# Sparse attention: the two heads of an output tile handled as one unit, their matmuls alternating

## The chip, the cores and the metric

The kernel runs on one core of one Trainium2 chip. The metric is the device time of the program in microseconds (us); lower is better.

## The reference, cut to what matters

The program is one layer of a decoder trunk on 256 tokens of width 2048 in float32: a first feed-forward, a mixer of three branches (a short gated convolution, a sparse attention, a cross-attention into 256 memory tokens), an output projection, and a second feed-forward. The part that the change touches is the sparse attention. It has 16 heads of width 64 in 4 groups. Each head adds up three gated terms:

```
p_c = masked_softmax(q . k_c * scale)          # 15 compressed keys
o_s = softmax(q . k_sel * scale) . v_sel       # selected blocks: at 256 tokens all of them, causal
o_w = softmax(q . k_win * scale) . v_win       # window: at 256 tokens the full causal prefix
o   = g0 * (p_c . v_c) + g1 * o_s + g2 * o_w   # sigmoid gates
```

At this length both the selected branch and the window branch are full causal attention over 256 tokens, with different keys and values.

## The kernel before, in words

**The main stream.** All projections are streams of 128x128 weight tiles, eight to a chunk (512 KB). `Stream.fetch` (L134 to L144) loads a chunk as `wraw`; ScalarE rounds it to `whi` (L143), VectorE takes the rest as `wlo` (L144). `proj` (L213) then issues two matmuls for each weight tile into a PSUM tile `psw` of two banks: `whi` against 512 columns (L232, both halves of the operand) and `wlo` against 256 columns (L233). `evac` (L238) empties `psw` with one ScalarE and one VectorE instruction.

**Side work.** Everything else runs as Python generators that are stepped between weight tiles. A `tick` (L203) first advances each active generator by one step, in order, and then takes the next one from `queue` and runs its first step. `proj` calls `tick` at fixed places of a group of weight tiles. While the sparse attention is computed, the stream goes through 32 groups of 24 weight tiles (gate and branch projections of the convolution and memory branches, L820 to L834); three groups of four have one tick at their end, and the fourth has one in its middle and one at its end. So ticks lie 24 or 12 weight tiles apart. When the program is built, a scheduler orders the instructions of each engine by their place in the program and by when it reckons their operands to be ready. The order on each engine is fixed from then on.

**The sparse attention.** Head pairs: output tile j (of 8) holds two heads, g = 0 on partitions 0 to 63 and g = 1 on 64 to 127. For each j, branch and g there is one `causal_unit` (L637), 32 in all. Its first step makes the scores into one bank (tag "sc", one buffer), with two matmuls that read 64 partitions: 128 columns for the first 128 tokens (L645), 256 for the others (L646). Mask and maximum on VectorE (L652, L655), exponent on ScalarE (L657), and the scaling on VectorE (L660 to L663) follow. The second step, a tick later, transposes the three 128x128 blocks (L667, bank tag "pt", two buffers) and copies them out (`T`, L669). The third, another tick later, adds the values into a half of the partitions of `on` (tag "o"), with one matmul of 256 columns (L672) and one of 128 (L673). For the first unit of an output tile, `begin` (L681) starts `on` with the compressed branch for both heads (L685). The fourth unit of a tile splits `on` into operand parts. `comp_attention` (L605), four in all, makes the compressed probabilities of four heads: eight score matmuls of 15 columns (L613), a small softmax, and in its second step two transposes (L633).

A float32 matmul appears in the trace as two passes, each a weight load and a matmul instruction, so L645 x2 is one matmul. A transpose is one pass.

At a tick in the steady state three units are in work, so TensorE gets: values of one, transposes of the next, scores of a third, and then goes on with the stream.

Of the kernel before, what the change touches and what calls it, by code (L numbers as in the profile page):

```python
# [17 lines left out]
P = 128  # L18
S = 256
# [13 lines left out]
def order(group, late):  # L33
    """(member, k tile, first, last) of a group of output tiles; the last `late` k tiles come last for all,
    or all members take turns ("k")."""
    out = []
    if late == "k":
        n = len(group[0])
        out = [(j, kts[i], i == 0, i == n - 1) for i in range(n) for j, kts in enumerate(group)]
    elif late:  # L40
        for j, kts in enumerate(group):
            out += [(j, k, i == 0, False) for i, k in enumerate(kts[:len(kts) - late])]
        for j, kts in enumerate(group):
            rest = kts[len(kts) - late:]
            out += [(j, k, False, i == late - 1) for i, k in enumerate(rest)]
    else:
        for j, kts in enumerate(group):
            out += [(j, k, i == 0, i == len(kts) - 1) for i, k in enumerate(kts)]
    return out
# [41 lines left out]
def cuts(n, ramp=()):  # L91
    """(first tile, tiles) of the chunks of a stream of n tiles; small ones first where nothing is loaded yet."""
# [14 lines left out]
# columns of the packed parameters  # L107
# [39 lines left out]
class Trunk:  # L147
    def __init__(self, ctx, tc, a):
# [18 lines left out]
        # the tensor engine's clock rises while the first loads are on their way  # L167
# [26 lines left out]
    def spawn(self, gen):  # L194
        """Start side work at once; each further step comes with a tick."""
# [17 lines left out]
    def proj(self, stream, group, late, X, ticks=0, before=None, fold=False):  # L213
        """PSUM tiles [128, 2 members, 512]: (Wh + Wl) @ hi in the first half, Wh @ lo in the second
        (or in the first too, with `fold`)."""
# [31 lines left out]
    def split(self, src, pool=None, tag="h", scale=None):  # L247
        """hi / lo parts of src as a tile [128, 2, 256]."""
# [13 lines left out]
    def norm_parts(self, x, pr, gain, pool, tag):  # L262
        """Operand parts of gain * x for k tiles 2pr, 2pr + 1."""
        return [self.split(x[:, j, :], pool, tag, scale=self.p(gain, 2 * pr + j)) for j in range(2)]

    def norm_sum(self, x):
        """The running sum of squares."""
# [13 lines left out]
    def norm_end(self):  # L281
        """r = rsqrt(mean square + eps): token-major [128, 2] and spread over partitions [128, 256]."""
# [26 lines left out]
    def head_scale(self, ps, out, r, width, post):  # L309
        """out = post * r * rsqrt(r^2 * ss / width + eps), all [128 tokens, 2, n]; ss in PSUM."""  # L310
# [12 lines left out]
    def squares(self, t, fold=False):  # L323
        """Squares of a pair of tiles; with `fold`, both added in the first."""
# [6 lines left out]
    def wide_stats(self, sq):  # L331
        """Sums over the partitions of the first tile of sq: PSUM [128 tokens, 2, 1]."""
# [7 lines left out]
    def half_stats(self, sq):  # L340
        """Sums over each half of each tile of sq: PSUM [128 tokens, 2, 4 = (tile, half)]."""
# [8 lines left out]
    def to_tokens(self, t, out):  # L350
        """[128 f, 2, 256 tokens] -> [128 tokens, 2, 2 tiles, 128 f]."""
# [51 lines left out]
    def mem_kv(self, kvp, x1):  # L403
        """Keys [128 d, 2, 256] and values [128 tokens, 2, 2, 128] of the memory heads; also the first operand."""
# [89 lines left out]
    def nsa_key(self, t, r, gain, out):  # L494
        """rms norm of 64-wide heads, feature-major: out = t * gain * r * rsqrt(...)."""
# [20 lines left out]
    def nsa_gates(self, t, rb, G):  # L516
        """sigmoid of the branch gates, token-major [128, 2, head, branch]; rows with no compressed key get 0 there."""
# [13 lines left out]
    def compress(self, t, rb, kind, w1, finish):  # L531
        """silu(windows @ w1) as hidden [128, 2, 4 groups, 15], handed to the generator `finish`."""
# [8 lines left out]
        # R[(parity, d), k tile, group, window]  # L541
# [49 lines left out]
    def comp_values(self, hid, out):  # L591
        """out [128 = (head slot, 32), head slot, group, 64]: block diagonal copies of v_c."""
# [12 lines left out]
    def comp_attention(self, a, g, Q, CQ, kc, G, Pp, ptc):  # L605
        """Compressed-branch probabilities of four heads, transposed: [128 = (head slot, 32), 256 tokens]."""
        nc = self.nc
        ps = self.psa.tile([P, 512], F32, name="scc", tag="sc")
        pv = ps[:, :120].rearrange("p (t i n) -> p t i n", t=2, i=4)
        sl = slice(64 * g, 64 * g + 64)  # L610
        for i in range(4):
            for tt in range(2):
                nc.tensor.matmul(pv[:, tt, i, :], Q[2 * a + i // 2][sl, i % 2, tt * P:(tt + 1) * P], kc[sl, a, :],  # L613
                                 start=True, stop=True)
        shp = [P, 2, 4, 15]
        L = self.ap.tile(shp, F32, name="Lc", tag="Lc", bufs=2)
        nc.vector.tensor_tensor(L, pv, CQ[a][:, :, :, g].unsqueeze(3).to_broadcast(shp), op=ALU.mult)
        cm = self.p("cmask").rearrange("p (t n) -> p t n", t=2).unsqueeze(2).to_broadcast(shp)
        nc.vector.tensor_tensor(L, L, cm, op=ALU.min)
        m = self.sm.tile([P, 2, 4], F32, name="mc", tag="mc")  # L620
        nc.vector.tensor_reduce(m, L, axis=AX.X, op=ALU.max)
        nc.vector.tensor_tensor(L, L, m.unsqueeze(3).to_broadcast(shp), op=ALU.subtract)
        nc.scalar.activation(L, L, AF.Exp)
        s = self.sm.tile([P, 2, 4], F32, name="scm", tag="scm")
        nc.vector.tensor_reduce(s, L, axis=AX.X, op=ALU.add)
        nc.vector.reciprocal(s, s)
        h0 = 8 * a + 4 * g
        nc.vector.tensor_tensor(s, s, G[:, :, h0:h0 + 4, 0], op=ALU.mult)
        nc.vector.tensor_tensor(Pp[:, :, :, 0:15], L, s.unsqueeze(3).to_broadcast(shp), op=ALU.mult)
        yield  # L630
        pt = self.psa.tile([P, 512], F32, name="ptc", tag="pt", bufs=2)
        for tt in range(2):
            nc.tensor.transpose(pt[:, tt * P:(tt + 1) * P], Pp[:, tt].rearrange("p i n -> p (i n)"), self.ident)  # L633
        ptc[a, g] = self.yp.tile([P, S], F32, name="ptc%d%d" % (a, g), tag="ptc%d" % g)
        nc.vector.tensor_copy(ptc[a, g], pt[:, :S])

    def causal_unit(self, j, g, br, Q, CQ, k, v, G, begin, end):  # L637
        """One head against the full causal prefix, added into o[64 g : 64 g + 64] of its pair of heads."""
# [3 lines left out]
        head = 8 * a + 4 * g + i  # L642
        sl = slice(64 * g, 64 * g + 64)
        ps = self.psa.tile([P, 512], F32, name="sc", tag="sc")
        nc.tensor.matmul(ps[:, 0:P], q[sl, jj, 0:P], k[sl, a, 0:P], start=True, stop=True)  # L645
        nc.tensor.matmul(ps[:, P:3 * P], q[sl, jj, P:S], k[sl, a, :], start=True, stop=True)  # L646
        L = self.ap.tile([P, 512], F32, name="L", tag="L", bufs=2)
        nm = self.sm.tile([P, 2], F32, name="nb", tag="nb")
        ssum = self.sm.tile([P, 2], F32, name="ssum", tag="ssum")
        cols = (slice(0, P), slice(P, 3 * P))  # L650
        for qt, mk in ((0, self.p("mask", P, P)), (1, self.p("mask"))):
            nc.vector.scalar_tensor_tensor(L[:, cols[qt]], ps[:, cols[qt]], c[:, qt, i, g:g + 1], mk,  # L652
                                           op0=ALU.mult, op1=ALU.min)
        for qt in range(2):
            nc.vector.tensor_reduce(nm[:, qt:qt + 1], L[:, cols[qt]], axis=AX.X, op=ALU.max, negate=True)  # L655
        for qt in range(2):
            nc.scalar.activation(L[:, cols[qt]], L[:, cols[qt]], AF.Exp, bias=nm[:, qt:qt + 1],  # L657
                                 accum_out=ssum[:, qt:qt + 1])
        f = self.sm.tile([P, 2], F32, name="f", tag="f")
        nc.vector.reciprocal(f, ssum)  # L660
        nc.vector.tensor_tensor(f, f, G[:, :, head, br], op=ALU.mult)
        for qt in range(2):
            nc.vector.tensor_scalar(L[:, cols[qt]], L[:, cols[qt]], f[:, qt:qt + 1], None, op0=ALU.mult)  # L663
        yield
        pt = self.psa.tile([P, 512], F32, name="pt", tag="pt", bufs=2)
        for n in range(3):
            nc.tensor.transpose(pt[:, n * P:(n + 1) * P], L[:, n * P:(n + 1) * P], self.ident)  # L667
        T = self.ap.tile([P, 512], F32, name="T", tag="T", bufs=2)
        nc.scalar.activation(T[:, :3 * P], pt[:, :3 * P], AF.Copy)  # L669
        yield  # L670
        o = begin()
        nc.tensor.matmul(o[sl, 0:S], v[:, 0, a, sl], T[:, 0:S], start=False, stop=False)  # L672
        nc.tensor.matmul(o[sl, P:S], v[:, 1, a, sl], T[:, S:3 * P], start=False, stop=br == 2)  # L673
        end(o)

    def nsa_pair(self, j, Q, cq, kv, vcz, ptc, G, out):
        """The four units of a pair of heads, which share one output tile."""
# [11 lines left out]
        def end(o):  # L689
            state["n"] += 1  # L690
            if state["n"] == 4:
                out[j] = self.split(o[:, 0:S], self.yp, "yn%d" % j)

        for br, k, v in kv:
            for g in range(2):
                self.queue.append(self.causal_unit(j, g, br, Q, cq, k, v, G, begin, end))

# [254 lines left out]
```

## Time and profile before

| | |
|---|---|
| runs | 2514.23, 2518.75, 2528.36 us; median 2518.75 us |
| span of the profiled execution | 2527.0 us; the nearest of the three times, 2528.36 us, lies 1.36 us above it |
| TensorE matmul busy | 2514.2 us (99% of the span) |
| VectorE, ScalarE busy | 1594.6 us (63%), 1208.3 us (48%) |
| mean granted TensorE clock | 0.995 |

The span runs from the first to the last instruction of the program. Busy time of TensorE is modelled from its starts, so spacing between starts tells more of it than durations do.

### The profile page before, as it was taken

What the parts mean: (1) busy time and instruction counts of PE and PEld (TensorE: products, weight loads), DVE (VectorE), ACT (ScalarE), POOL (GpSimd) and SP (SyncE); (2) the same over time, 40 slices, a digit from 0 to 9 for tenths busy, and PEclk for the clock granted to TensorE, in tenths of its full rate; (3) what the DMA queues carried; (4) which work ended last, traced back from release to release, by engine and by line L of the source; (5) the groups of instructions that cost most, each with busy time, mean ns of one, the idle gap of its engine ahead of it and who ended that gap; (6) DMA issues with size and microseconds to landing.
All of it is one profiled execution on the core that took longest, in us unless ns stands there. A gap on an engine that the chain in (4) does not pass through costs nothing.

```text
span 2527.0 us, 36419 instructions
## 1 busy us (share of the span) xinstructions
PE 2514.2 (99%) x14388; PEld 2172.1 (86%) x14388; DVE 1594.6 (63%) x2190; ACT 1208.3 (48%) x1660; POOL 33.6 (1%) x42
## 2 busy tenths in 40 slices
PE   9999999999999999999999999999999999999999
PEld 7888888888888888888878778888888888888888
DVE  8666666666667666545666666766666566666665
ACT  7544444444445444333454544555544444444443
POOL 0000000000000000010000000000000000000000
PEclk9999999999999999999999999999999999999999
DMA  7556566566657645654444445566565555656564
GB/s 265 183 188 191 190 192 189 187 191 191 191 188 222 212 158 167 192 175 147 146 136 132 142 134 179 188 193 205 184 189 184 187 188 184 188 186 185 188 186 159
DMA packets 128348, 459.98 MB, mean 182 GB/s; under 512 B 14512, under 2 KB 15024, under 8 KB 127664
## 3 DMA queue, kind: packets, MB, share of 16 engines
q1 hardware_dynamic: 127152, 454.50, 57.0%
q0 software_dynamic: 1024, 3.14, 0.4%
q8 instruction: 113, 1.85, 0.3%
q14 instruction: 59, 0.48, 0.0%
HBM read 452.35 MB, written 4.19 MB: 181 GB/s over the span
## 4 chain that ended last, share of the span: by engine, by line
PE 98%; DMA 1%; DVE 0%; ACT 0%; POOL 0%; SPq 0%; issue 0%; DVEq 0%; ACTq 0%
PE psw L232 61%; PE psw L233 31%; PE phid L553 1%; PE on L672 1%; PE pt L667 1%; PE sc L646 1%; PE sc L645 1%; PE scc L613 0%; PE sc L464 0%; PE on L673 0%; PE o L489 0%; DMA xin<-memT 0%; DMA Ev<-t 0%; PE pso L232 0%; DMA Ek<-t 0%; PE psw L230 0%
## 5 line engine op out<-in xcount | busy, mean ns | idle before, releaser
L232 PE MATMUL psw<-xs,whi 128*128 128x512 f32 x4432 | 1568.0, 398 | 0.0
L144 DVE TENSOR_TENSOR wlo<-wraw,whi 128x1024 fp32r<-128x1024 f32 (+1 forms) x844 | 1031.1, 1222 | 789.8 <-ACT whi L143 788.7
L143 ACT ACTIVATE whi<-wraw 128x1024 fp32r<-128x1024 f32 (+1 forms) x844 | 891.7, 1057 | 1075.7 <-PE psw L232 679.3
L233 PE MATMUL psw<-xs,wlo 128*128 128x256 f32 x4432 | 1245.5, 281 | 0.0
L232 PEld LDWEIGHTS psw<-xs,whi 128*128 128x128 f32 x4432 | 834.2, 188 | 205.1 <-issue 7.1
L233 PEld LDWEIGHTS psw<-xs,wlo 128*128 128x128 f32 x4432 | 840.4, 190 | 0.1
L232 PE MATMUL psw<-h,whi 128*128 128x512 f32 x2122 | 747.7, 396 | 3.3 <-ACT whi L143 3.3
L233 PE MATMUL psw<-h,wlo 128*128 128x256 f32 x2144 | 602.1, 281 | 0.2 <-DVE wlo L144 0.2
L232 PEld LDWEIGHTS psw<-h,whi 128*128 128x128 f32 x2122 | 398.3, 188 | 96.9 <-ACT whi L143 4.7
L233 PEld LDWEIGHTS psw<-h,wlo 128*128 128x128 f32 x2144 | 405.7, 189 | 1.1 <-DVE wlo L144 0.9
L244 DVE TENSOR_TENSOR t<-psw,t 128x512 f32<-128x512 f32 x233 | 159.1, 683 | 9.0 <-ACT t L243 9.0
L243 ACT ACTIVATE t<-psw 128x512 f32<-128x512 f32 x233 | 135.5, 582 | 27.5 <-PE psw L233 27.1
L252 ACT ACTIVATE h<-s 128x256 fp32r<-128x256 f32 x88 | 36.8, 418 | 114.2 <-DVE s L371 114.2
L253 DVE TENSOR_TENSOR h<-s,h 128x256 fp32r<-128x256 f32 x88 | 37.4, 425 | 42.1 <-ACT h L252 42.1
L368 DVE TENSOR_TENSOR t<-t,rb 128x512 f32<-128x512 f32 x88 | 60.9, 693 | 3.1
L657 ACT ACTIVATE L<-L,nb 128x128 f32<-128x128 f32 x64 | 28.6, 448 | 37.2 <-DVE nb L655 37.2
L232 PE MATMUL psw<-yn,whi 128*128 128x512 f32 x128 | 45.7, 395 | 0.0
L378 DVE SCALAR_TENSOR_TENSOR x<-t,x 128x512 f32<-128x512 f32 x63 | 43.6, 692 | 2.2
L371 DVE TENSOR_TENSOR s<-s,t 128x256 f32<-128x256 f32 x88 | 36.8, 419 | 1.0 <-ACT s L370 1.0
L233 PE MATMUL psw<-yn,wlo 128*128 128x256 f32 x128 | 36.0, 282 | 0.0
L370 ACT ACTIVATE s<-t 128x256 f32<-128x256 f32 x88 | 35.3, 401 | 0.0
L232 PEld LDWEIGHTS psw<-yn,whi 128*128 128x128 f32 x128 | 24.1, 188 | 5.7
(189 smaller groups left out, 806.1 us busy)
## 6 DMA issues: line engine op xcount, KB each, us to landing
wraw<-w_ffn SPq DMA_DIRECT2D x528, 512.0 KB, 3.5
wraw<-w_mix SPq DMA_DIRECT2D x282, 512.0 KB, 3.5
wraw<-w_mem SPq DMA_DIRECT2D x31, 512.0 KB, 4.8
xin<-memT SPq DMA_DIRECT2D x8, 256.0 KB, 5.1
x<-xT SPq DMA_DIRECT2D x8, 256.0 KB, 4.8
xspill<-x POOLq DMA_DIRECT2D x8, 256.0 KB, 3.4
xin<-xspill SPq DMA_DIRECT2D x8, 256.0 KB, 3.6
w<-w1k SPq DMA_DIRECT2D x2, 1024.0 KB, 5.6
```

The source lines that it names most:

```text
L143: nc.scalar.activation(self.wh[:, :w], raw[:, :w], AF.Copy)
L144: nc.vector.tensor_tensor(self.wl[:, :w], raw[:, :w], self.wh[:, :w].bitcast(F32), op=ALU.subtract)
L232: nc.tensor.matmul(ps, wh, x.rearrange("p a n -> p (a n)"), start=first, stop=False)
L233: nc.tensor.matmul(ps[:, :S], wl, x[:, 0, :], start=False, stop=last)
L243: nc.scalar.activation(t[:, part], ps[:, part, S:], AF.Copy)
L244: nc.vector.tensor_tensor(t[:, part], ps[:, part, :S], t[:, part], op=ALU.add)
L252: nc.scalar.activation(h[:, 0, :], src, AF.Copy)
L253: nc.vector.tensor_tensor(h[:, 1, :], src, h[:, 0, :].bitcast(F32), op=ALU.subtract)
L368: nc.vector.tensor_tensor(t, t, self.both(rb), op=ALU.mult)
L370: nc.scalar.activation(s, t[:, 0, :], AF.Silu)
L371: nc.vector.tensor_tensor(s, s, t[:, 1, :], op=ALU.mult)
L378: nc.vector.scalar_tensor_tensor(xp[pr][:, part], t[:, part], 0.5, xp[pr][:, part], op0=ALU.mult, op1=ALU.add)
```

## The change

`causal_unit` becomes `causal_pair`, which handles both heads of an output tile for one branch: 16 units in place of 32. The four score matmuls alternate between the two heads, that is between the two halves of the partitions that they read, and write two banks (one "sc", one of the two "pt"). The value matmuls alternate between the two halves of `on`. The softmax instructions of the two heads are the same as before and follow one another, the second head's mask and maximum ahead of the first head's scaling. `comp_attention` likewise takes both g, 2 units in place of 4. After each unit an empty one is put in the queue, so that a pair takes two ticks, as two units did. The transposes of both heads come in the tick after the scores, the values in the tick after that, which is also the tick of the next pair's scores. The diff also takes comments and docstrings out; they are not shown.

```diff
-    def comp_attention(self, a, g, Q, CQ, kc, G, Pp, ptc):
-        ps = self.psa.tile([P, 512], F32, name="scc", tag="sc")
-        pv = ps[:, :120].rearrange("p (t i n) -> p t i n", t=2, i=4)
-        sl = slice(64 * g, 64 * g + 64)
+    def comp_attention(self, a, Q, CQ, kc, G, pps, ptc):
+        tiles = [self.psa.tile([P, 512], F32, name="scc", tag=tag, bufs=n) for tag, n in (("sc", 1), ("pt", 2))]
+        pvs = [ps[:, :120].rearrange("p (t i n) -> p t i n", t=2, i=4) for ps in tiles]
         for i in range(4):
             for tt in range(2):
-                nc.tensor.matmul(pv[:, tt, i, :], Q[2 * a + i // 2][sl, i % 2, tt * P:(tt + 1) * P], kc[sl, a, :],
-                                 start=True, stop=True)
+                for g in range(2):
+                    sl = slice(64 * g, 64 * g + 64)
+                    nc.tensor.matmul(pvs[g][:, tt, i, :], Q[2 * a + i // 2][sl, i % 2, tt * P:(tt + 1) * P],
+                                     kc[sl, a, :], start=True, stop=True)
...
-    def causal_unit(self, j, g, br, Q, CQ, k, v, G, begin, end):
-        head = 8 * a + 4 * g + i
-        sl = slice(64 * g, 64 * g + 64)
-        ps = self.psa.tile([P, 512], F32, name="sc", tag="sc")
-        nc.tensor.matmul(ps[:, 0:P], q[sl, jj, 0:P], k[sl, a, 0:P], start=True, stop=True)
-        nc.tensor.matmul(ps[:, P:3 * P], q[sl, jj, P:S], k[sl, a, :], start=True, stop=True)
+    def causal_pair(self, j, br, Q, CQ, k, v, G, begin, end):
+        sls = [slice(64 * g, 64 * g + 64) for g in range(2)]
+        pss = [self.psa.tile([P, 512], F32, name="sc", tag=tag, bufs=n) for tag, n in (("sc", 1), ("pt", 2))]
+        for qt in range(2):
+            for g, sl in enumerate(sls):
+                nc.tensor.matmul(pss[g][:, cols[qt]], q[sl, jj, qt * P:(qt + 1) * P], k[sl, a, 0:(qt + 1) * P],
+                                 start=True, stop=True)
+        Ls = []
+        for g in range(2):
...
+            Ls.append((L, ssum, head))
+        for L, ssum, head in Ls:
...
         yield
-        pt = self.psa.tile([P, 512], F32, name="pt", tag="pt", bufs=2)
-        for n in range(3):
-            nc.tensor.transpose(pt[:, n * P:(n + 1) * P], L[:, n * P:(n + 1) * P], self.ident)
+        Ts = []
+        for L, _, _ in Ls:
+            pt = self.psa.tile([P, 512], F32, name="pt", tag="pt", bufs=2)
+            for n in range(3):
+                nc.tensor.transpose(pt[:, n * P:(n + 1) * P], L[:, n * P:(n + 1) * P], self.ident)
...
         yield
         o = begin()
-        nc.tensor.matmul(o[sl, 0:S], v[:, 0, a, sl], T[:, 0:S], start=False, stop=False)
-        nc.tensor.matmul(o[sl, P:S], v[:, 1, a, sl], T[:, S:3 * P], start=False, stop=br == 2)
+        for sl, T in zip(sls, Ts):
+            nc.tensor.matmul(o[sl, 0:S], v[:, 0, a, sl], T[:, 0:S], start=False, stop=False)
+        for sl, T in zip(sls, Ts):
+            nc.tensor.matmul(o[sl, P:S], v[:, 1, a, sl], T[:, S:3 * P], start=False, stop=br == 2)
         end(o)
...
-            if state["n"] == 4:
+            if state["n"] == 2:
...
         for br, k, v in kv:
-            for g in range(2):
-                self.queue.append(self.causal_unit(j, g, br, Q, cq, k, v, G, begin, end))
+            self.queue.append(self.causal_pair(j, br, Q, cq, k, v, G, begin, end))
+            self.queue.append(iter(()))
...
         for ga in range(2):
-            for g in range(2):
-                self.queue.append(self.comp_attention(ga, g, Q, CQ, kc, G, pps[g], ptc))
+            self.queue.append(self.comp_attention(ga, Q, CQ, kc, G, pps, ptc))
+            self.queue.append(iter(()))
```

## Rows read from the trace of the kernel before

**Rows 1.** The page: busy time by engine, granted clock, chain by engine.

```profile
PE 2514.2 (99%) x14388; PEld 2172.1 (86%) x14388; DVE 1594.6 (63%) x2190; ACT 1208.3 (48%) x1660; POOL 33.6 (1%) x42
...
PEclk9999999999999999999999999999999999999999
...
PE 98%; DMA 1%; DVE 0%; ACT 0%; POOL 0%; SPq 0%; issue 0%; DVEq 0%; ACTq 0%
```

**Rows 2.** Waits of TensorE: us in total, times, longest; the largest of five.

```profile
PE psw L232 <- ACT whi L143: 3.3, 3, 2.2
```

**Rows 3.** Timeline of TensorE, one steady tick: start us, length us.

```profile
1277.64 0.28 PE L233 MATMUL psw<-xs,wlo 128*128 128x256 f32 x1
...
1278.00 0.28 PE L233 MATMUL psw<-xs,wlo 128*128 128x256 f32 x1
1278.21 0.65 PE L672 MATMUL on<-T,vw 128*64 128x256 f32 x2
1278.69 0.38 PE L673 MATMUL on<-T,vw 128*64 128x128 f32 x2
1279.01 0.55 PE L667 MATMUL pt<-par,L 128*128 128x128 f32 x3
1279.48 0.49 PE L645 MATMUL sc<-ks,nq 64*128 64x128 f32 x2
1279.81 0.59 PE L646 MATMUL sc<-ks,nq 64*128 64x256 f32 x2
...
1280.67 0.28 PE L233 MATMUL psw<-xs,wlo 128*128 128x256 f32 x1
```

**Rows 4.** Timeline of TensorE, a tick that starts an output tile.

```profile
1225.52 0.65 PE L685 MATMUL on<-ptc,vcz 128*64 128x256 f32 x4
1226.00 0.59 PE L672 MATMUL on<-T,vs 128*64 128x256 f32 x2
1226.43 0.38 PE L673 MATMUL on<-T,vs 128*64 128x128 f32 x2
```

**Rows 5.** Timeline of TensorE, stream around a tick with values alone.

```profile
1525.78 0.28 PE L233 MATMUL psw<-h,wlo 128*128 128x256 f32 x1
...
1527.12 0.28 PE L233 MATMUL psw<-xs,wlo 128*128 128x256 f32 x1
```

**Rows 6.** Timeline of TensorE, stream around a tick with scores alone.

```profile
1373.33 0.28 PE L233 MATMUL psw<-xs,wlo 128*128 128x256 f32 x1
...
1374.73 0.28 PE L233 MATMUL psw<-xs,wlo 128*128 128x256 f32 x1
```

**Rows 7.** Timeline of TensorE, two transposes inside the stream.

```profile
1376.14 0.28 PE L233 MATMUL psw<-h,wlo 128*128 128x256 f32 x1
...
1376.48 0.38 PE L633 MATMUL ptc<-par,pp 128*128 128x128 f32 x2
...
1377.06 0.28 PE L233 MATMUL psw<-h,wlo 128*128 128x256 f32 x1
```

**Rows 8.** Timeline of TensorE, a compressed-branch unit, behind two transposes (L633).

```profile
1194.15 0.28 PE L233 MATMUL psw<-xs,wlo 128*128 128x256 f32 x1
...
1194.57 1.95 PE L613 MATMUL scc<-kc,nq 64*128 64x15 f32 x16
...
1196.80 0.28 PE L233 MATMUL psw<-xs,wlo 128*128 128x256 f32 x1
```

**Rows 9.** Timeline of VectorE: first and last softmax work of one unit.

```profile
1280.44 0.74 DVE L652 SCALAR_TENSOR_TENSOR L<-sc,cq,par 128x128 f32<-128x128 f32 x2 [0.96 <-PE sc L646]
...
1282.89 0.55 DVE L663 TENSOR_SCALAR L<-L,f 128x128 f32<-128x128 f32 x2
```

**Rows 10.** Windows: length, busy by engine (PE, PEld, DVE, ACT, POOL), granted clock, DMA share, GB/s.

```profile
1187.10:1190.50 3.40, 3.40 (x12) 2.92 (x12) 2.86 (x9) 0.31 (x1) 0.32 (x1) 0.51 0.13 51
...
1368.00:1371.40 3.40, 3.40 (x13) 2.91 (x12) 2.94 (x7) 0.00 (x0) 0.00 (x0) 0.51 0.35 90
1205.00:1526.50 321.50, 321.50 (x1775) 255.48 (x1774) 214.08 (x465) 159.97 (x310) 2.48 (x1) 0.99 0.44 138
```

More of the change, by code (lines that the diff above doesn't have):

```diff
@@ L615, in comp_attention @@
         shp = [P, 2, 4, 15]
-        L = self.ap.tile(shp, F32, name="Lc", tag="Lc", bufs=2)
-        nc.vector.tensor_tensor(L, pv, CQ[a][:, :, :, g].unsqueeze(3).to_broadcast(shp), op=ALU.mult)
         cm = self.p("cmask").rearrange("p (t n) -> p t n", t=2).unsqueeze(2).to_broadcast(shp)
[L619 to L629, printed above, removed]
-        yield
-        pt = self.psa.tile([P, 512], F32, name="ptc", tag="pt", bufs=2)
@@ L632, in comp_attention @@
[L632 to L635, printed above, removed]
-    def causal_unit(self, j, g, br, Q, CQ, k, v, G, begin, end):
+        for g in range(2):
+            L = self.ap.tile(shp, F32, name="Lc", tag="Lc", bufs=2)
+            nc.vector.tensor_tensor(L, pvs[g], CQ[a][:, :, :, g].unsqueeze(3).to_broadcast(shp), op=ALU.mult)
+            nc.vector.tensor_tensor(L, L, cm, op=ALU.min)
+            m = self.sm.tile([P, 2, 4], F32, name="mc", tag="mc")
+            nc.vector.tensor_reduce(m, L, axis=AX.X, op=ALU.max)
+            nc.vector.tensor_tensor(L, L, m.unsqueeze(3).to_broadcast(shp), op=ALU.subtract)
+            nc.scalar.activation(L, L, AF.Exp)
+            s = self.sm.tile([P, 2, 4], F32, name="scm", tag="scm")
+            nc.vector.tensor_reduce(s, L, axis=AX.X, op=ALU.add)
+            nc.vector.reciprocal(s, s)
+            h0 = 8 * a + 4 * g
+            nc.vector.tensor_tensor(s, s, G[:, :, h0:h0 + 4, 0], op=ALU.mult)
+            nc.vector.tensor_tensor(pps[g][:, :, :, 0:15], L, s.unsqueeze(3).to_broadcast(shp), op=ALU.mult)
@@ L639, in causal_unit @@
+        yield
+        for g in range(2):
+            pt = self.psa.tile([P, 512], F32, name="ptc", tag="pt", bufs=2)
+            for tt in range(2):
+                nc.tensor.transpose(pt[:, tt * P:(tt + 1) * P], pps[g][:, tt].rearrange("p i n -> p (i n)"), self.ident)
+            ptc[a, g] = self.yp.tile([P, S], F32, name="ptc%d%d" % (a, g), tag="ptc%d" % g)
+            nc.vector.tensor_copy(ptc[a, g], pt[:, :S])
+    def causal_pair(self, j, br, Q, CQ, k, v, G, begin, end):
         nc = self.nc
@@ L641, in causal_unit @@
         q, c = Q[j // 2], CQ[a]
-        head = 8 * a + 4 * g + i
-        sl = slice(64 * g, 64 * g + 64)
-        ps = self.psa.tile([P, 512], F32, name="sc", tag="sc")
-        nc.tensor.matmul(ps[:, 0:P], q[sl, jj, 0:P], k[sl, a, 0:P], start=True, stop=True)
-        nc.tensor.matmul(ps[:, P:3 * P], q[sl, jj, P:S], k[sl, a, :], start=True, stop=True)
-        L = self.ap.tile([P, 512], F32, name="L", tag="L", bufs=2)
-        nm = self.sm.tile([P, 2], F32, name="nb", tag="nb")
-        ssum = self.sm.tile([P, 2], F32, name="ssum", tag="ssum")
+        sls = [slice(64 * g, 64 * g + 64) for g in range(2)]
@@ L650, in causal_unit @@
+        pss = [self.psa.tile([P, 512], F32, name="sc", tag=tag, bufs=n) for tag, n in (("sc", 1), ("pt", 2))]
         cols = (slice(0, P), slice(P, 3 * P))
-        for qt, mk in ((0, self.p("mask", P, P)), (1, self.p("mask"))):
-            nc.vector.scalar_tensor_tensor(L[:, cols[qt]], ps[:, cols[qt]], c[:, qt, i, g:g + 1], mk,
-                                           op0=ALU.mult, op1=ALU.min)
         for qt in range(2):
-            nc.vector.tensor_reduce(nm[:, qt:qt + 1], L[:, cols[qt]], axis=AX.X, op=ALU.max, negate=True)
@@ L656, in causal_unit @@
[L656 to L663, printed above, removed]
-        yield
@@ L665, in causal_unit @@
-        pt = self.psa.tile([P, 512], F32, name="pt", tag="pt", bufs=2)
-        for n in range(3):
-            nc.tensor.transpose(pt[:, n * P:(n + 1) * P], L[:, n * P:(n + 1) * P], self.ident)
-        T = self.ap.tile([P, 512], F32, name="T", tag="T", bufs=2)
-        nc.scalar.activation(T[:, :3 * P], pt[:, :3 * P], AF.Copy)
+            for g, sl in enumerate(sls):
+                nc.tensor.matmul(pss[g][:, cols[qt]], q[sl, jj, qt * P:(qt + 1) * P], k[sl, a, 0:(qt + 1) * P],
+                                 start=True, stop=True)
@@ new lines, in causal_pair @@
+        Ls = []
+        for g in range(2):
+            ps = pss[g]
+            head = 8 * a + 4 * g + i
+            L = self.ap.tile([P, 512], F32, name="L", tag="L", bufs=2)
+            nm = self.sm.tile([P, 2], F32, name="nb", tag="nb")
+            ssum = self.sm.tile([P, 2], F32, name="ssum", tag="ssum")
+            for qt, mk in ((0, self.p("mask", P, P)), (1, self.p("mask"))):
+                nc.vector.scalar_tensor_tensor(L[:, cols[qt]], ps[:, cols[qt]], c[:, qt, i, g:g + 1], mk,
+                                               op0=ALU.mult, op1=ALU.min)
+            for qt in range(2):
+                nc.vector.tensor_reduce(nm[:, qt:qt + 1], L[:, cols[qt]], axis=AX.X, op=ALU.max, negate=True)
+            for qt in range(2):
+                nc.scalar.activation(L[:, cols[qt]], L[:, cols[qt]], AF.Exp, bias=nm[:, qt:qt + 1],
+                                     accum_out=ssum[:, qt:qt + 1])
+            Ls.append((L, ssum, head))
@@ new lines, in causal_pair @@
+        for L, ssum, head in Ls:
+            f = self.sm.tile([P, 2], F32, name="f", tag="f")
+            nc.vector.reciprocal(f, ssum)
+            nc.vector.tensor_tensor(f, f, G[:, :, head, br], op=ALU.mult)
+            for qt in range(2):
+                nc.vector.tensor_scalar(L[:, cols[qt]], L[:, cols[qt]], f[:, qt:qt + 1], None, op0=ALU.mult)
+        yield
+        Ts = []
[3 more added lines that the diff above has]
+                nc.tensor.transpose(pt[:, n * P:(n + 1) * P], L[:, n * P:(n + 1) * P], self.ident)
+            T = self.ap.tile([P, 512], F32, name="T", tag="T", bufs=2)
+            nc.scalar.activation(T[:, :3 * P], pt[:, :3 * P], AF.Copy)
+            Ts.append(T)
```

## The prediction

> **What bounds the kernel now.** I read the page first. TensorE is busy for 99% of the span, the chain that ended last is TensorE for 98%, and the clock is full in nearly every slice [rows 1]. The waits of TensorE come to 8.8 us over five entries, the largest 3.3 us [rows 2]. Nothing else holds this kernel up: VectorE has 63% and ScalarE 48%. In the stretch of the sparse attention it is no different: in 321.5 us VectorE works 214.08 and ScalarE 159.97 [rows 10]. So what the change is worth is the TensorE time that the side work inserts into the stream, read from the spacing of starts in the timeline.
>
> The stream's own pace is one weight tile (L232, L233) in 0.36 us, from L233 to L233 [rows 3]. A steady tick pushes the next L233 away by 1280.67 - 1278.00 = 2.67 us, so it costs 2.31 us [rows 3]. It holds three things, and some ticks show each by itself, with 0.35 us taken off for the stream. Values alone: 1527.12 - 1525.78 - 0.35 = 0.99 us [rows 5]. Scores alone: 1374.73 - 1373.33 - 0.35 = 1.05 us [rows 6]. Two transposes in the midst of the stream, over two weight tiles: 1377.06 - 1376.14 - 0.71 = 0.21 us, 0.11 us each [rows 7]. Three are 0.33 us, and the parts sum to 2.37 us against 2.31.
>
> What values and scores cost beyond their columns is the second thing to see. In a tick that starts an output tile, L672 x2 comes behind another value matmul and takes 1226.43 - 1226.00 = 0.43 us, 0.215 us for a pass of 256 columns [rows 4]; as the first piece of a tick it takes 1278.69 - 1278.21 = 0.48 us, and L673 x2, with half the columns, takes 0.32 us up to the transposes instead of 0.21 [rows 3]. A unit's values (two passes of 256 columns, two of 128) thus stream for 0.64 us. So 0.35 us of the 0.99 are entering and leaving: a gap of some 0.10 us at each end and a weight load that nothing hides. Scores have the same columns and 0.40 us of the same kind. Transposes have none (0.11 us for 128 columns is what such a pass of the values streams for); they use the array in the shape of the stream.
>
> **The change part by part.** All of it is on the path, since TensorE is the bound.
>
> Values of a pair. Eight passes in place of twice four, and neighbours now write different halves of `on`. The trace has this pattern: L685 alternates the halves, and its four passes of 256 columns take 1226.00 - 1225.52 = 0.48 us [rows 4], as long as the two passes of L672 on one half [rows 3]. The halves run at the same time. Bounds: a pair streams for 0.64 us if all of it pairs up, 1.28 if none. I take 0.64, because L685 is the same instruction on the same halves.
>
> Scores of a pair. Neighbours now read different halves of the partitions and write different banks. No row shows two such matmuls side by side. Bounds: 0.64 us (both at once) and 1.28 us (one after the other). The nearest row is again L685, so I take 0.64, with less trust. The Trainium skill (TensorE: Matmul & The Clock Gate, Part 3, "Measured speedup vs the span model") gives 3.07 times for four row tiles at once, 0.77 of the ideal. No run here shows that; with 0.64/0.77 a pair's scores would take 0.19 us more, 3 us in all, and the sum below would end at 2485.
>
> Fewer entries. A pair took two ticks of 2.31 us, 4.62 us. Now its even tick holds values and scores, 0.99 + 1.05 less one leaving and entering that fall together (a gap of 0.10 and a load of 0.10): 1.84 us. Its odd tick holds six transposes in the stream's own shape, 0.66 us. That is 4.62 - 1.84 - 0.66 = 2.12 us for a pair and 33.9 us for 16. With scores one after the other it is 0.64 less, 1.48 us and 23.7; with values too, 0.84 us and 13.4. If the falling together gives nothing, each loses 3 us.
>
> Compressed branch. One unit's 16 passes of 15 columns cost 1196.80 - 1194.15 - 0.35 - 0.22 = 2.08 us, 0.112 each and an entry [rows 8]; at 15 columns that is the weight loads. Four units become two with alternating halves: 4.2 us saved if the loads of the two halves run together, 0.5 us if only an entry is saved. I take 4.2 with the scores and 0.5 without. After two of the four such bursts the clock was granted at 0.51 for 3.4 us, the lower level (1.2 GHz) [rows 10]; one such stretch loses some 1.7 us. Two bursts instead of four, shorter or longer, may bring none or three of these: plus or minus 3 us, taken at nothing.
>
> The L685 passes, the splits, the softmax instructions and the copies are as many as before. Their cover is the stream on TensorE: with some 37 us gone, VectorE's 214 us stand in 285 us, 75%.
>
> What comes later. In the tick after the scores both heads' transposes are due. One head's softmax takes from 1280.44 to 1283.44, 3.0 us [rows 9]; two heads in turn at most 6.0 us, as VectorE does the second head's mask while ScalarE does the first head's exponent. Ticks are 24 or 12 weight tiles apart, 8.5 or 4.3 us of stream. At the wide ones there is room; at the narrow ones (two of five, so 6 or 7 of 16 pairs) L is up to 1.7 us late. TensorE takes its instructions in order, so all of the stream is behind a waiting transpose. But the order is made when the program is built, and late transposes are placed inside the stream, as the two of L633 between an L232 and its L233 [rows 7]. Bounds 0 and 12 us; I take 2. The first head's values wait for both heads' copies, a tick later, which is free. On VectorE the evacuation of `psw` stands behind up to 1.5 us more softmax; its second buffer gives it a group of 24 weight tiles.
>
> Sum: 33.9 + 4.2 - 2 = 36.1 us. From the span that gives 2527.0 - 36.1 = 2490.9; the span lies 8.25 us above the median of the runs shown, and from the median it is 2518.75 - 36.1 = 2482.6.
>
> **Rivals.** (1) Passes on different halves of the partitions don't run at once: 23.7 + 0.5 - 2 = 22.2 us, 2496.5. For it: no row shows them together. Against it: the gap before L645 is there although L667 ahead of it is plain (the array is put in another shape), and L685 pairs up for columns.
>
> (2) The softmax of two heads in one go becomes a wait: TensorE stands at the transposes of the 7 narrow ticks for 1.7 us, 12 us in all, so 38.1 - 12 = 26 us, 2492.6. Each tick's margin is for it; the freedom of the order is against it. The Trainium skill says as much in TensorEngine Tiling, "PSUM Bottleneck": packing speeds up TensorE and not the emptying of PSUM, which may then be the limit. The trace has VectorE at 67% there, which speaks against a limit, not against single waits.
>
> (3) The other side: every change between halves of the partitions costs what entering another shape costs, some 0.21 us of gap and load. There are 8 score passes in each of 16 pairs and 32 in each of two compressed units, 192 changes. 24.2 - 192 x 0.21 = -16 us: 2535. It cancels the gain at 0.13 us a change, and is slower by over 0.5% from 0.19. Against it: L685 changes halves at no price. For it: nothing beyond the missing row.
>
> (4) The change doesn't do what it says, since the order made at build time parts the alternating matmuls (as L645 and L646 could be parted by transposes that come due). Then entries come back, 0.35 to 0.40 us each, and half of the pairing goes: about 10 us gained, 2509, within 0.5%.
>
> **How the numbers follow.** 0.5% is 12.6 us, about what three runs of this kernel can tell from no change. All at once as summed: 0.60, 2482.6, by itself 2475 to 2488. Rival 1: 0.17. Rival 2: 0.10. Rival 3: 0.06. Rival 4: 0.07. The first three cases are faster: 0.87. Rival 4 is the same: 0.07. Rival 3 is slower: 0.06. The range reaches down to 2474 (no late transposes, no stretches at the lower clock, and some 3 us of spread between runs) and up to 2500 (rival 1 with the spread), which leaves out rivals 3 and 4 and the far ends.
>
> **What would show it.** A pair of heads' four value matmuls (eight passes) spanning 0.7 us; L645 and L646 successors, eight passes, within some 0.75 us and not 1.4; even ticks that cost 1.84 us and odd ones 0.66; a compressed unit's 32 passes in about 1.9 us. TensorE waits named for the transposes or for L on VectorE would show rival 2, gaps inside the run of alternating scores rival 3, stream matmuls between the scores of a pair rival 4. The forecast is wrong if scores don't pair up, or if TensorE's waits grow by more than some 10 us.

## The result, and the profile after

The changed kernel takes 2486.69 us in the median (2483.02 to 2491.16, four runs) against 2516.82 us (2514.23 to 2528.36, four runs): a ratio of 0.9879, 95% interval 0.9848 to 0.9909. That is 30.1 us less; the interval reaches from 23 to 38 us less, and the forecast was 36.1 us less, 2482.6 us. It was run twice more beside the last experiments, with ratios of 0.9814 (0.9782 to 0.9847) and 0.9819 (0.9785 to 0.9853). The first interval and the second only just fail to meet; the steps of 13.8 us that the last section shows move single runs, and with them the medians of a few.

The page after, the lines that answer to [rows 1]:

```profile
span 2489.4 us, 36404 instructions
...
PE 2476.5 (99%) x14388; PEld 2153.6 (87%) x14388; DVE 1591.1 (64%) x2190; ACT 1206.1 (48%) x1660; POOL 32.8 (1%) x42
...
PE 98%; DMA 1%; DVE 0%; ACT 0%; POOL 0%; SPq 0%; issue 0%; DVEq 0%; ACTq 0%
```

TensorE is the bound as before, with the same number of passes, 14388, and its waits come to 8.8 us as before. The even tick, values and scores of two heads, in the timeline of TensorE (start, length):

```profile
1284.11 0.28 PE L233 MATMUL psw<-xs,wlo 128*128 128x256 f32 x1
1284.32 0.65 PE L688 MATMUL on<-T,vw 128*64 128x256 f32 x4
1284.80 0.39 PE L690 MATMUL on<-T,vw 128*64 128x128 f32 x4
1285.12 0.93 PE L652 MATMUL sc<-ks,nq 64*128 64x128 f32 x8
1285.97 0.50 PE L232 MATMUL psw<-xs,whi 128*128 128x512 f32 x1
1286.31 0.28 PE L233 MATMUL psw<-xs,wlo 128*128 128x256 f32 x1
```

Set this beside [rows 3], where the stream's next matmul is this one:

```profile
1280.33 0.50 PE L232 MATMUL psw<-xs,whi 128*128 128x512 f32 x1
```

L688 x4 takes 0.48 us up to the next piece, as L672 x2 did for one head; the eight passes of scores take 0.85 us from their start to the stream's next matmul, as the four of L645 and L646 did (1280.33 - 1279.48). Two heads stream in the time of one, on rows of the array (scores) and on columns (values). The tick costs 1286.31 - 1284.11 - 0.35 = 1.85 us. The odd tick, six transposes in the stream:

```profile
1279.28 0.28 PE L233 MATMUL psw<-h,wlo 128*128 128x256 f32 x1
1279.40 0.82 PE L681 MATMUL pt<-par,L 128*128 128x128 f32 x6
...
1280.29 0.28 PE L233 MATMUL psw<-xs,wlo 128*128 128x256 f32 x1
```

It costs 1280.29 - 1279.28 - 0.35 = 0.66 us. A compressed unit of both halves, which answers to [rows 8]:

```profile
1200.43 1.96 PE L615 MATMUL scc<-kc,nq 64*128 64x15 f32 x32
1202.33 0.50 PE L232 MATMUL psw<-xs,whi 128*128 128x512 f32 x1
```

32 passes take 1.90 us up to the stream. Before, 16 took 1196.46 - 1194.57 = 1.89 us; the matmul of the stream behind them was

```profile
1196.46 0.50 PE L232 MATMUL psw<-xs,whi 128*128 128x512 f32 x1
```

The best measure of the changed part is the stretch from the first compressed score to the first matmul that uses the branch's result (`psw<-yn`). The stream's work in it is the same in every kernel here. As windows, first of the kernel before, then of the changed one:

```profile
1185.15:1557.98 372.83, 372.83 (x2066) 300.25 (x2065) 245.78 (x519) 180.66 (x338) 4.12 (x2) 0.99 0.45 141
```

```profile
1200.43:1534.15 333.72, 333.72 (x2065) 280.40 (x2065) 242.20 (x519) 176.80 (x338) 3.27 (x2) 0.99 0.51 158
```

The stretch is 39.1 us shorter, with the same passes. The rest of the two profiled executions has unchanged code, but not the same time: the part before the stretch took 15.3 us longer (1200.43 against 1185.15) and the part behind it 13.8 us less (2489.4 - 1534.15 = 955.2 against 2527.0 - 1557.98 = 969.0). The spans differ by 39.1 + 13.8 - 15.3 = 37.6 us. The last section shows what this unsteadiness is; it is why the experiments are read from this stretch and from ticks, and from totals only where these are large enough. The stretch itself isn't quite steady: the changed kernel had 332.30 and 333.54 us in its two later traces, so a difference of about one us in it says nothing.

### The profile page after: what moved, and what is told of

Read it like the earlier page. It is cut to its first block, busy times and chain, and to the rows that moved or that the text cites. A ratio compares the mean times of both kernels' runs of the same rounds, so it can differ in the third digit from the quotient of the medians.

```text
span 2489.4 us, 36404 instructions
## 1 busy us (share of the span) xinstructions
PE 2476.5 (99%) x14388; PEld 2153.6 (87%) x14388; DVE 1591.1 (64%) x2190; ACT 1206.1 (48%) x1660; POOL 32.8 (1%) x42
## 3 DMA queue, kind: packets, MB, share of 16 engines
q8 instruction: 113, 1.85, 0.3%
## 4 chain that ended last, share of the span: by engine, by line
PE 98%; DMA 1%; DVE 0%; POOL 0%; ACT 0%; SPq 0%; issue 0%; DVEq 0%; ACTq 0%
PE psw L232 62%; PE psw L233 32%; PE phid L553 1%; PE sc L652 1%; PE pt L681 0%; PE on L688 0%; PE sc L464 0%; DMA wraw<-w_mem 0%; PE pso L232 0%; PE o L489 0%; DMA Ek<-t 0%; DMA Ev<-t 0%; PE psw L230 0%; PE pstat L347 0%; PE on L702 0%; PE scc L615 0%
```

## The experiments

**1. Nothing alternates.** The pairs stay, each head's matmuls follow one another.

```diff
-        for qt in range(2):
-            for g, sl in enumerate(sls):
+        for g, sl in enumerate(sls):
+            for qt in range(2):
                 nc.tensor.matmul(pss[g][:, cols[qt]], ...)
...
         for sl, T in zip(sls, Ts):
             nc.tensor.matmul(o[sl, 0:S], v[:, 0, a, sl], T[:, 0:S], start=False, stop=False)
-        for sl, T in zip(sls, Ts):
             nc.tensor.matmul(o[sl, P:S], v[:, 1, a, sl], T[:, S:3 * P], start=False, stop=br == 2)
...
-        for i in range(4):
-            for tt in range(2):
-                for g in range(2):
+        for g in range(2):
+            for i in range(4):
+                for tt in range(2):
```

> The changed kernel with its pairs as units, but nothing alternates: all scores of head 0, then all of head 1; the same for the values and for the compressed scores. Theory A (halves run at the same time as long as the order of starts lets them; starts keep program order): scores of a pair stream for about 0.86 us instead of 0.64 (the second head starts as soon as the first head's second matmul has started), values 1.07 instead of 0.64, a compressed unit about 3.6 us instead of 2.0. An even tick costs 1.85 + 0.22 + 0.43 = 2.50 us, so +10.4 us over 16 pairs and +3.3 us for two compressed units: about 2500 us, half of the way back from 2487. Theory B (only neighbours that start together overlap, otherwise one after the other): even tick 3.13 us, about 2511 us. Theory C (the gain comes from fewer units and entries alone, and the hardware pairs up whatever order it finds): even tick stays at 1.85 us, 2487 us.

Ratio 0.9916 (0.9894 to 0.9938), 2492.52 us; the stretch is 337.39 us, 3.7 us more than the changed kernel's (the ratios lie further apart than that, but their intervals overlap). The even tick in the timeline:

```profile
1284.74 0.28 PE L233 MATMUL psw<-xs,wlo 128*128 128x256 f32 x1
1284.95 0.66 PE L688 MATMUL on<-T,vw 128*64 128x256 f32 x4
1285.43 0.40 PE L689 MATMUL on<-T,vw 128*64 128x128 f32 x4
1285.75 0.93 PE L652 MATMUL sc<-ks,nq 64*128 64x128 f32 x8
...
1286.95 0.28 PE L233 MATMUL psw<-xs,wlo 128*128 128x256 f32 x1
```

It costs 1286.95 - 1284.74 - 0.35 = 1.86 us, 0.01 more than with alternation. (In ticks that also start an output tile it is 2.34 us against 2.28, 0.06 more.) In the program the order is L688 and L689 of head 0, then L688 and L689 of head 1, yet all four passes of L688 stand ahead of those of L689. The scheduler that orders the instructions at build time isn't the cause: in all 16 pairs the list of TensorE instructions in the built program has L688 and L689 for the first half of `on`, then both for the other. A window of 0.05 us at the start of the tick shows two passes of L688 under way, one of each head; in the kernel before, such a window shows one pass of L672:

```profile
1284.95 0.44 PE L688 MATMUL on<-T,vw 128*64 128x256 f32 x2
```

So theories A and B fall, and C holds for scores and values: TensorE starts head 1's matmul on the free half past head 0's second one, which waits for its own half. C doesn't hold for the compressed scores, eight matmuls to a half:

```profile
1199.37 3.32 PE L615 MATMUL scc<-kc,nq 64*128 64x15 f32 x32
1202.62 0.50 PE L232 MATMUL psw<-xs,whi 128*128 128x512 f32 x1
```

3.25 us up to the stream in place of 1.90. With two such units, 2.7 of the 3.7 us are there, and some 0.5 us in the ticks that start an output tile; the rest is within what the stretch varies by.

**2. Only the values in turn.** The middle part of the diff above, alone.

> Scores and compressed scores alternate as in the changed kernel; only the values are head 0's two matmuls, then head 1's two. Theory A: even tick 1.85 + 0.43 = 2.28 us, 16 times 0.43 is +6.9 us, about 2494 us. Theory B: even tick 2.49 us, +10.2 us, about 2497 us. Theory C: no change, 2487 us.

Ratio 0.9885 (0.9842 to 0.9927), 2487.27 us. Theory C again: the tick with L688, L689 and L652 runs from 1280.08 to 1282.29, 1.86 us of cost:

```profile
1280.08 0.28 PE L233 MATMUL psw<-xs,wlo 128*128 128x256 f32 x1
...
1282.29 0.28 PE L233 MATMUL psw<-xs,wlo 128*128 128x256 f32 x1
```

**3. A short score matmul beside a long one.**

```diff
-        for qt in range(2):
-            for g, sl in enumerate(sls):
+        for g, qt in ((0, 0), (1, 1), (0, 1), (1, 0)):
+            for sl in (sls[g],):
```

> The pair's scores alternate, but a short matmul (128 columns) of one head stands beside a long one (256) of the other. Theory A (each half goes on by itself): both halves still have 384 columns, streaming stays at 0.64 us, the even tick at 1.85 us. Theory D (two halves move in step, the shorter waits for the longer): 0.86 us, even tick 2.07 us, +3.5 us in all.

One run, 2487.27 us. The eight passes take as long as with equal partners, 1282.60 - 1281.75 = 0.85 us up to the stream. Each half goes on by itself; D falls.

```profile
1281.75 0.92 PE L652 MATMUL sc<-ks,nq 64*128 64x128 f32 x8
1282.60 0.50 PE L232 MATMUL psw<-xs,whi 128*128 128x512 f32 x1
```

**4. A pair at every tick.** The empty unit behind each pair is left out.

```diff
             self.queue.append(self.causal_pair(j, br, Q, cq, k, v, G, begin, end))
-            self.queue.append(iter(()))
```

> The changed kernel without the empty units between pairs: a pair starts at every tick, so that values, transposes and scores of three pairs share a tick, and the softmax of two heads comes twice as often, in half the stretch. Entries theory: the transposes again part values from scores, so a tick costs 1.85 + 0.66 + about 0.15 = 2.66 us in place of 2.51 for a pair, +2.4 us in all, about 2489 us, with no waits of TensorE. Softmax theory (rival 2 of the prediction): VectorE has some 6 us of softmax beside 5.5 us of stream work per 8.5 us of stream at a wide tick, and more than it can do at a narrow one; TensorE waits at transposes or for weight rests, 1 to 3 us a pair: 2505 us or more.

Ratio 0.9932 (0.9907 to 0.9958), 2497.65 us; the stretch is 346.34 us, 12.6 us more than with the empty units. Both theories missed. TensorE's waits name no softmax instruction, but a tick costs 1247.46 - 1244.07 - 0.35 = 3.04 us and not 2.66:

```profile
1244.07 0.28 PE L233 MATMUL psw<-xs,wlo 128*128 128x256 f32 x1
1244.28 0.65 PE L688 MATMUL on<-T,vw 128*64 128x256 f32 x4
1244.76 0.39 PE L690 MATMUL on<-T,vw 128*64 128x128 f32 x4
1245.08 0.88 PE L681 MATMUL pt<-par,L 128*128 128x128 f32 x6
1245.89 1.30 PE L652 MATMUL sc<-kw,nq 64*128 64x128 f32 x8
1247.12 0.50 PE L232 MATMUL psw<-xs,whi 128*128 128x512 f32 x1
1247.46 0.28 PE L233 MATMUL psw<-xs,wlo 128*128 128x256 f32 x1
```

The scores take 1.23 us up to the stream, 0.38 more than in the changed kernel. A window that ends at 1246.20 shows two passes of L652 so far, one head's; ScalarE is then copying the transposes out (first row TensorE, then ScalarE, copies of both heads merged):

```profile
1245.89 0.49 PE L652 MATMUL sc<-kw,nq 64*128 64x128 f32 x2
```

```profile
1245.73 0.87 ACT L683 ACTIVATE T<-pt 128x384 f32<-128x384 f32 x2
```

The second head's scores need one of the two "pt" banks, and both hold transposes of this tick until ScalarE has copied the first. Of the eight weight loads of these scores the trace has a semaphore wait on one alone, the second head's first, and the semaphore is ScalarE's; it starts at 1246.27, and ScalarE's copy for the first head, 0.49 us from 1245.73, ends at 1246.22. Head 0's second score matmul stands behind it in the built program and starts only at 1246.28, 0.39 us behind the first. In the ticks where the build put it ahead, it starts 0.33 us behind the first, as in the changed kernel. So here TensorE did not go past a matmul that waits for another engine. No run with a third bank was tried.

Of the 12.6 us, twelve ticks that hold all three pieces account for some 6 (0.53 each). The second compressed unit stands behind six transposes here and takes 3.34 us up to the stream instead of 1.89, 1.5 us more. In it the clock fell to 0.50, the lower level, until about 1305.2 us, which the changed kernel doesn't have there; in the 5.6 us of that behind the burst the stream's weight tiles lie 0.64 us apart instead of 0.35, and by an estimate 2.5 us are lost. The remaining 2 us are not assigned.

**5. Two banks, but one half.** The second head's scores read head 0's partitions, so its probabilities are those of head 0's query and key.

```diff
-            for g, sl in enumerate(sls):
+            for g, sl in enumerate(sls[:1] * 2):
                 nc.tensor.matmul(pss[g][:, cols[qt]], ...)
```

> The changed kernel, but the second head's score matmuls read the first head's half of the partitions, into their own bank as before (so the second head's probabilities are those of the first head's query and key). Order, banks, columns and entries stay. Theory A2 (matmuls run at the same time when they read different halves): the eight passes now stream one after the other, 1.28 us in place of 0.64; even tick 1.85 + 0.64 = 2.49 us, the stretch of the sparse attention 10.2 us longer than the changed kernel's 333.7 us. Rival (neighbours run at the same time because they write different banks, or because two instructions are open at once): even tick stays at 1.85 us.

One run, 2509.96 us. The passes stream one after the other, 1284.51 - 1283.00 = 1.51 us up to the stream against 0.85, and the stretch is 343.34 us, 9.6 us more. It is the halves that run at once, and not the two banks or two open instructions.

```profile
1283.00 1.57 PE L652 MATMUL sc<-ks,nq 64*128 64x128 f32 x8
1284.51 0.50 PE L232 MATMUL psw<-xs,whi 128*128 128x512 f32 x1
```

**6. How far ahead TensorE looks.** Blocks of two in the first compressed unit, of four in the second.

```diff
-        for i in range(4):
-            for tt in range(2):
-                for g in range(2):
+        n = 2 if a == 0 else 4
+        for m0 in range(0, 8, n):
+            for g in range(2):
+                for m in range(m0, m0 + n):
+                    i, tt = m // 2, m % 2
```

> The compressed scores in blocks: the first unit takes two matmuls of one half, then two of the other; the second takes four and four. Everything else as in the changed kernel. Look-ahead theory (each half holds one running and one waiting matmul; a third for the same half stops the issue for both; 0.224 us a matmul, 0.19 us of entry): blocks of two 8 x 0.224 + 0.19 = 1.98 us, as alternating; blocks of four 10 x 0.224 + 0.19 = 2.43 us; eight and eight would be 14 x 0.224 + 0.19 = 3.33, which is what the run without alternation had (4.235 - 0.894 = 3.34 us). Rival (strict neighbours): blocks of two pair up only at their borders, 2.9 us, and blocks of four 3.4 us. Rival (looks ahead without limit): 1.98 us for both.

One run, 2490.88 us. From the start of the burst to the stream:

```profile
1198.37 1.98 PE L617 MATMUL scc<-kc,nq 64*128 64x15 f32 x32
1200.28 0.50 PE L232 MATMUL psw<-xs,whi 128*128 128x512 f32 x1
...
1348.89 2.48 PE L617 MATMUL scc<-kc,nq 64*128 64x15 f32 x32
1351.30 0.80 PE L232 MATMUL psw<-xs,whi 128*128 128x512 f32 x1
```

1.91 us for blocks of two, as alternating (1.90); 2.41 for blocks of four, 0.51 more where the look-ahead theory gave 0.45; 3.25 for eight. The built program has the blocks as they are written here. One running and one waiting matmul for each half fits all three (2.43 and 3.33 us were reckoned for the longer ones); strict neighbours and a reach without limit fit neither of them.

**7. The changed kernel again, and the same idea elsewhere.** The compression (`phid`) has 128 passes of 60 columns in four bursts of 32. At the full clock a pass takes 0.11 us (the second burst below), as one of 15 columns does [rows 8], so I take it to be bound by weight loads of 128 columns. Its matmuls are split into two column halves that alternate.

```diff
-                nc.tensor.matmul(ps[:, f, :60], w[:, k, :], R[:, k].rearrange("p g n -> p (g n)"),
-                                 start=k == 0, stop=k == 15)
+                for c in (slice(0, 64), slice(64, 128)):
+                    nc.tensor.matmul(ps[c, f, :60], w[:, k, c], R[:, k].rearrange("p g n -> p (g n)"),
+                                     start=k == 0, stop=k == 15)
```

> The changed kernel itself, to have it on the same chip as the next one. All theories: ratio 0.988 to 0.986 to the kernel before; stretch of the sparse attention 333.7 us in the profile.

> The changed kernel, and in the compression each matmul of 60 columns (four bursts of 32 passes, bound by weight loads of 128 columns: 3.5 us at the full clock, 5.3 to 5.9 us where the clock fell) is split into two column halves, 64 weights each, that alternate. If loads of the two halves run at the same time, as those of the compressed scores do: 64 passes in 32 x 0.055 us = 1.8 us a burst and 0.3 us of entry, four bursts 8.4 us in place of 18.2: some 9 us less than the changed kernel, 2478 us, ratio about 0.984. If loads run one after the other: 64 x 0.055 = 3.5 us and the entries on top, 1 us more than the changed kernel.

The changed kernel: 2486.08 us, 0.9814 (0.9782 to 0.9847), below the 0.986 to 0.988 expected. With the split: 2474.56 us, 0.9794 (0.9758 to 0.9829). A burst at the full clock, the second one in the first trace of the changed kernel, and then the first with the split:

```profile
1089.67 3.68 PE L553 MATMUL phid<-Rk,w 128*128 128x60 f32 x32
1093.18 1.01 PE L347 MATMUL pstat<-par,sq 128*128 128x2 f32 x8
```

```profile
1058.05 2.08 PE L554 MATMUL phid<-Rk,w 128*64 128x60 f32 x64 [1.04 <-DVE Rk L546]
1060.06 0.50 PE L232 MATMUL psw<-xs,whi 128*128 128x512 f32 x1
```

2.01 us in place of 3.51, with twice the passes: weight loads of two halves run at the same time. The clock gives more. In the changed kernel it fell in the first and the third burst, which took 5.90 and 5.31 us (in the trace beside the split one only in the third); in the split kernel's trace it fell in none. Windows of the changed kernel, of the split one over the first two bursts, and of the run with quarters below, whose third burst is split as well (the granted clock is the third number from the end):

```profile
1076.70:1086.90 10.20, 10.20 (x42) 9.42 (x41) 2.60 (x3) 0.69 (x2) 0.00 (x0) 0.50 0.56 193
```

```profile
1058.00:1070.00 12.00, 11.82 (x173) 10.60 (x174) 7.00 (x10) 3.49 (x5) 0.33 (x1) 1.00 0.68 233
```

```profile
1112.10:1115.50 3.40, 3.40 (x38) 3.00 (x34) 3.21 (x4) 0.00 (x0) 0.00 (x0) 0.50 0.44 119
```

So in these traces the fall is rarer with the split, and not ruled out by it. From the first burst to the first compressed score, with the same work between them, the changed kernel's trace beside the split one took 1195.51 - 1072.89 = 122.6 us, and the split one 1168.77 - 1058.05 = 110.7 us: 11.9 us less, where some 9 were expected.

**8. Quarters.** On top, compressed scores in four tiles of 64 rows and 64 columns.

```diff
             for tt in range(2):
-                for g in range(2):
+                for c in range(2):
+                    for g in range(2):
...
+                        t0 = tt * P + 64 * c
+                        nc.tensor.matmul(pvs[g][64 * c:64 * c + 64, tt, i, :], Q[2 * a + i // 2][sl, i % 2, t0:t0 + 64],
+                                         kc[sl, a, :], start=True, stop=True)
```

> The run with the compression split into column halves, and in addition each compressed score matmul split into two column halves, so that four matmuls with 64 rows and 64 columns of weights each stand side by side (64 passes a burst instead of 32). If four quarters run at the same time: loads of 64 columns, 16 x 0.055 + 0.17 = 1.05 us a burst from its start to the next matmul of the stream, in place of 1.90; 1.7 us less for the two bursts, about 9 us less than the changed kernel in all. If only two of them do: 1.9 us a burst as before. If four collide in order or loads: 3.6 us a burst.

> The changed kernel beside it on the same chip: ratio 0.981 to 0.988 to the kernel before.

With quarters 2472.2 us, 0.9794 (0.9762 to 0.9826); the changed kernel beside it 2484.37 us, 0.9819 (0.9785 to 0.9853). The burst takes 1323.38 - 1322.33 = 1.05 us, as expected of four at once.

```profile
1322.33 1.12 PE L618 MATMUL scc<-kc,nq 64*64 64x15 f32 x64
1323.38 0.50 PE L232 MATMUL psw<-xs,whi 128*128 128x512 f32 x1
```

Both extended kernels have medians some 12 us below the changed kernel's on the same chip, but their intervals overlap with its, so the totals alone don't settle that they beat it; the bursts and the part of the program around them are shorter in the traces (run 7; with the quarters 1173.86 - 1060.32 = 113.5 us against 123.3 in the changed kernel beside it). The quarters' 1.7 us can't be seen in a total.

## Why the prediction was right, step by step

**The bound.** Right: TensorE stays at 99%, and what left the side work left the time.

**Values and scores at once.** Right in size: 0.64 us of streaming for two heads, which was taken from L685 for the values and on trust for the scores. Run 5 puts the scores' share at 9.6 us by undoing it. The same wasn't tried for the values, whose columns are equal in number. The 0.77 of the ideal that the prediction worked out for four row tiles from the Trainium skill (TensorE: Matmul & The Clock Gate, Part 3, "Measured speedup vs the span model") isn't seen with two halves: they lose nothing measurable (0.85 us for eight passes and for four).

**What brings them together.** Here the prediction's picture was off, though no term was. It took neighbouring matmuls to be what pairs up, and gave rival 4 a chance on that ground. Runs 1 and 2 show that the alternation inside a pair is worth 0.01 us a tick (0.06 where an output tile starts). What counts is that both heads come in the same tick; TensorE goes past one matmul that waits for its half. The prediction's sentence that TensorE takes its instructions in order is too strict there. Rival 4 itself didn't come about: the eight passes of scores stand together, and alternate, in all 16 pairs. The written order matters where a half has a longer run, in the compressed units: 1.35 us each.

**Fewer entries.** Right: 1.85 and 0.66 us measured, 1.84 and 0.66 reckoned, 2.11 us a pair or 33.8 us. Of these 20 are the pairing and 13 the entries, by the prediction's division; the 13 aren't shown by a run of their own, only by the ticks.

**Compressed branch.** 4.2 us reckoned. The cost of a unit of two is that of a unit of one, so two of 2.08 us are gone. Run 1 puts 2.7 us of it on the order. One stretch of the lower clock is left in the window, against two [rows 10], which by the prediction's price gives 1.7 us more (the changed kernel's trace beside run 7 has none in its stretch and is 1.4 us shorter there):

```profile
1203.00:1206.40 3.40, 3.40 (x12) 2.88 (x11) 3.40 (x16) 0.50 (x2) 0.00 (x0) 0.50 0.00 0
```

**Late transposes.** 2 us allowed. TensorE's waits in the stretch name L on VectorE before a weight load of a transpose for 1.6 us in all:

```profile
PEld pt L681 <- DVE L L675: 1.6, 5, 0.3
```

At narrow ticks the transposes stand apart inside the stream, as [rows 7] suggested. Rival 2 had its wait in the right place and at an eighth of its price, 1.6 us and not 12.

Sum: 33.8 + 4.2 + 1.7 - 1.6 = 38.1 us, against 39.1 in the stretch. The medians differ by less, 30.1 us in the first comparison and 40 us in the other two (2526.43 to 2486.08, 2524.71 to 2484.37); with the unsteadiness below, the forecast of 36.1 lies among them. That the first median came as near as 4 us owes something to luck; the ticks and the stretch are what bears the prediction out.

**The other rivals.** Rival 1 falls with the eight passes in 0.85 us, rival 3 too: there is no gap among them, and neighbours that change halves start together.

## What to carry to other kernels

Where TensorE is the bound, bring the matmuls that use half of the array's rows or columns into the same place of its queue, one half beside the other: here they streamed and loaded weights at the same time, and one entry into another shape of the array served both. Runs of two matmuls on one half needed no interleaving, longer ones did. Count the banks before packing tighter: a bank that is still being copied out is the next wait.

## What was not expected of the hardware

**TensorE starts matmuls past a waiting one.** Head 1's first matmul started beside head 0's first, although head 0's second stands ahead of it in the built program (run 1), with a reach of about one waiting matmul for each half (run 6). It did not start one past a matmul that waited for ScalarE (run 4).

**Weight loads pair up as well.** 32 passes of the compressed scores took what 16 took, and 64 half-width passes of the compression 2.01 us where 32 full ones took 3.51 us at the full clock (the changed kernel's second burst).

**The stream has two paces at the full clock.** The same code of a feed-forward ran at one of two paces in an execution, and the two feed-forwards choose independently. In 100 us of the first (500 to 600) and of the second (2100 to 2200), the kernel before had 579 and then 567 matmuls (the number in the first bracket):

```profile
500.00:600.00 100.00, 100.00 (x579) 88.19 (x578) 62.76 (x73) 48.03 (x63) 0.00 (x0) 1.00 0.61 191
2100.00:2200.00 100.00, 100.00 (x567) 86.70 (x567) 60.47 (x64) 44.94 (x53) 0.00 (x0) 1.00 0.59 188
```

and the changed kernel had them the other way round:

```profile
500.00:600.00 100.00, 100.00 (x569) 86.67 (x568) 62.13 (x72) 47.16 (x63) 0.00 (x0) 1.00 0.60 187
2100.00:2200.00 100.00, 100.00 (x579) 88.15 (x578) 61.23 (x68) 46.98 (x59) 0.00 (x0) 1.00 0.62 190
```

The run without alternation had the slower pace in both (567 and 567), the one with the split compression the faster in both (579 and 579), so all four combinations occur. With 2% between them, a feed-forward is 13.8 us longer or shorter (969.0 and 955.2 us behind the stretch). The changed kernel's runs beside the quarters show the step: 2468.36 and 2471.78, then 2482.77 to 2487.72 us. What chooses the pace stays open.
